# Windowed attention, mLSTM trunk: P^T V products in pairs, and K's low part on row halves in pairs

## The chip, the cores and the metric

One core of a Trainium2 chip runs the whole program. The metric is the device time of one execution in microseconds (us), the median of the runs; lower is better. The engines are named as in the profile: PE is TensorE's matmul, PEld its weight load, DVE is VectorE, ACT is ScalarE, POOL is GpSimd, SP issues DMAs.

## The reference, cut to what matters

Two sequences (2048 and 256 positions of 1024 values) go through an attention layer and an mLSTM layer, each with a residual, and a last RMS norm. The change lies in the attention layer alone:

```python
def window_attention_mixer(xn, w_in, sink, w_out):
    ...
    s = jnp.einsum('bnqgrd,bnkgd->bngrqk', qb, kb, preferred_element_type=jnp.float32)
    s = s * (ATTN_HEAD_DIM ** -0.5)
    ...
    m = jnp.maximum(jnp.max(s, axis=-1, keepdims=True), sk)
    p = jnp.exp(s - m)
    den = jnp.sum(p, axis=-1, keepdims=True) + jnp.exp(sk - m)
    p = (p / den).astype(vb.dtype)
    o = jnp.einsum('bngrqk,bnkgd->bnqgrd', p, vb).reshape(B, S, ATTN_WIDTH)
    return (o * jax.nn.silu(z)) @ w_out
```

There are 16 heads of 64 values in 4 groups; a group of 4 heads shares one K and one V. A block of 128 queries sees 3 blocks of keys (2 at the ends of a sequence).

## The kernel before, in words

The kernel works on 18 tiles of 128 positions (16 of the first sequence, 2 of the second), in stages: attention proper (`attn_core`), the gate and the output projection, and then the mLSTM layer. The change touches `attn_core` only.

In `attn_core` the projections (`project`, L376 to L378) multiply in three passes, since each operand is kept as a rounded high part and the rest as a low part: high by high, high by low, low by high. For a tile t there are four generators: `front(t + 2)` projects and rotates Q, K and V of a later tile; `scores` (letter s), `transposes` (p) and `values` (v) work on tile t. The string `AORDER` says in which order the program asks each for its next step. The tile framework then orders the instructions of each engine anew, with a model of their times, so that what stands next to what in an engine's queue is its choice; it may not break a dependence, and each buffer is one of a fixed number of copies.

`scores` (L489): for each of the 4 groups and each of its 4 heads, a PSUM tile S of 128 queries by up to 384 keys receives two passes, Q by KH (L500) and Q by KL (L501). Q holds 128 rows: for an even head rows 0 to 63 are the high part and rows 64 to 127 the low part, for an odd head the other way round (L454 to L457); KH and KL hold K's high and low part twice, in both row halves. So one pass of 128 rows gives the high and the low part of Q at once. There are two buffers "s", and in the last two tiles one more, "tq". VectorE adds the mask, takes the row's maximum and stores Sm (L503). After the fourth head it makes the group's nm (L508), ScalarE makes four exponentials in place (L514).

`transposes` (L522): for each group g and each key block j, four transposes (L528) fill one of two PSUM buffers "tr"; ScalarE (j = 0) or VectorE (else) copies it to PT (L531), one of NPT = 3 buffers. The order is all blocks of group 0, then all blocks of group 1, and so on.

`values` (L535): groups 2P and 2P + 1 share one PSUM tile o, one in partitions 0 to 63, the other in 64 to 127. For each block j and each of the two groups one product of V and PT (L541) is added; the operands are plain fp32, and each product stands as two passes in the trace. Then ScalarE copies o out (L544).

Of the kernel before, what the change touches and what calls it, by code (L numbers as in the profile page):

```python
# [11 lines left out]
F32 = mybir.dt.float32  # L12
# [31 lines left out]
NPT = 3  # L44
# [17 lines left out]
class Trunk:  # L62
# [330 lines left out]
    def attn_core(self):  # L393
        nc, tc, a = self.nc, self.tc, self.a
        with ExitStack() as st:
# [83 lines left out]
            def core(t):  # L479
# [9 lines left out]
                def scores():  # L489
                    for g in range(KVH):  # L490
                        mx = p.tile([128, 4], F32, tag="mx", name="mx", bufs=3)
                        Sg = []
                        for c in range(GRP):
                            h = g * GRP + c
                            Q = QS[t, h // 8]
                            q = Q[:, h % 2, (h % 8) // 2, :]
                            spare = NT - 2 <= t < SPT and c % 3 == 2
                            S = (pq if spare else ps).tile([128, 3, 128], F32, tag="tq" if spare else "s", name="s",
                                                           bufs=1 if spare else 2)
                            nc.tensor.matmul(S[:, :nk, :], q, KH[:, g, win, :], start=True, stop=False)  # L500
                            nc.tensor.matmul(S[:, :nk, :], q, KL[:, g, win, :], start=False, stop=True)  # L501
                            Sm = p.tile([128, 3, 128], F32, tag="Sm", name="Sm", bufs=NSM)
                            nc.vector.tensor_tensor_reduce(Sm[:, :nk], S[:, :nk], mask[:, t % 3, win, :], 1.0, MASKED,  # L503
                                                           ALU.add, ALU.max, mx[:, c:c + 1])
                            Sg.append(Sm)
# [16 lines left out]
                def transposes():  # L522
                    for g in range(KVH):
                        PTs[g] = []
                        for j in range(nk):
# [3 lines left out]
                            pt = p.tile([128, 512], F32, tag="PT", name="PT", bufs=NPT)  # L529
                            eng = nc.scalar.copy if j == 0 else nc.vector.tensor_copy  # L530
                            eng(pt[:], tp[:].rearrange("p c q -> p (c q)"))  # L531
                            PTs[g].append(pt)
                        yield

                def values():  # L535
                    for P in range(2):
                        o = ps.tile([128, 512], F32, tag="o", name="o", bufs=1)
                        for j in range(nk):
                            for gg in range(2):
                                g = 2 * P + gg  # L540
                                nc.tensor.matmul(o[gg * 64:(gg + 1) * 64, :], vof[sl[j]][:, g * HD:(g + 1) * HD],  # L541
                                                 PTs[g][j][:], start=j == 0, stop=j == nk - 1)
# [563 lines left out]
```

## Time and profile before

| | us |
|---|---|
| median of 3 runs | 2333.14 (2330.55 to 2336.04) |
| the profiled execution | 2326.69 |
| its span | 2324.8 |
| first and last product with V (L541) in it | 72.2 and 711.3 |
| mean granted clock of TensorE | 0.984 |

In the profile a row of a timeline holds start, duration, engine, line, operation, output and inputs, shape (rows by columns of the array, then the output) and count, and in brackets the engine's idle time before it with what ended it. TensorE overlaps its instructions: durations of matmuls are longer than the distance of their starts, and the distance is what a matmul costs. A window's row holds busy times of each engine, the granted clock, DMA share and GB/s.

### The profile page before, as it was taken

The page shows a single profiled execution, that of the slowest core. Times are in us where ns is not written, and L with a number is a line of the kernel's source. Part 1 is how long each engine was busy: PE and PEld are TensorE (multiplying, and loading weights), DVE is VectorE, ACT ScalarE, POOL GpSimd, SP SyncE. Part 2 cuts the span into 40 slices and gives each one's busy share as a digit, 9 for nine tenths or more (in the row PEclk, how much of TensorE's full clock was granted, in tenths as well). Part 3 has the DMA queues.
Part 4 walks back from the last instruction along what each step waited for, and adds up shares of the span by engine and source line. Part 5 has one row for each costly group of instructions (what it writes and reads, how often), then busy time and mean ns, then how long its engine had stood idle before and what let it go on. Part 6 is the DMA issues. An engine that isn't in the chain of part 4 may idle for free.

```text
span 2324.8 us, 32958 instructions
## 1 busy us (share of the span) xinstructions
PE 2239.7 (96%) x11102; PEld 1775.3 (76%) x11102; DVE 1564.6 (67%) x3403; ACT 1096.1 (47%) x2503; POOL 461.4 (20%) x392
## 2 busy tenths in 40 slices
PE   8999999999999998999899999999999996999998
PEld 7766666666666886888788899978877875888887
DVE  7575656565877779768655522397888786777784
ACT  6464545454765334445533411256454445554463
POOL 3212121212001221322000000012242234333320
PEclk9999999999999999999999999999999997999999
DMA  7111111111225447657533722354565457656642
GB/s 264 48 38 48 38 48 38 48 38 39 91 64 162 147 159 229 230 195 250 189 114 123 245 92 92 113 177 136 175 211 182 132 181 242 207 191 198 209 163 69
DMA packets 170281, 326.41 MB, mean 140 GB/s; under 512 B 18784, under 2 KB 21632, under 8 KB 170112
## 3 DMA queue, kind: packets, MB, share of 16 engines
q1 hardware_dynamic: 169968, 324.30, 42.0%
q8 instruction: 88, 1.44, 0.3%
q14 instruction: 81, 0.66, 0.1%
q10 hardware_dynamic: 144, 0.01, 0.0%
HBM read 235.34 MB, written 88.89 MB: 139 GB/s over the span
## 4 chain that ended last, share of the span: by engine, by line
PE 78%; DVE 8%; DMA 7%; issue 2%; ACT 2%; POOL 2%; SPq 0%; DVEq 0%; POOLq 0%; ACTq 0%
PE pj L378 9%; PE pj L376 9%; PE pj L377 9%; PE o L541 5%; PE pj L271 4%; PE pj L272 4%; PE pj L273 4%; PE ptp L528 4%; PE d L271 3%; PE d L272 3%; PE d L273 3%; PE c L272 3%; PE c L273 3%; PE c L271 3%; DMA qs<-rows 2%
## 5 line engine op out<-in xcount | busy, mean ns | idle before, releaser
L122 ACT CAST xhi<-rawx 128x512 fp32r<-128x512 f32 x372 | 228.6, 618 | 459.6 <-PE pj L377 109.0
L376 PE MATMUL pj<-whi,xhi 128*128 128x512 f32 (+2 forms) x1152 | 429.9, 374 | 8.5 <-ACT whi L167 6.9
L378 PE MATMUL pj<-whi,xlo 128*128 128x512 f32 (+2 forms) x1152 | 423.8, 373 | 5.8 <-DVE xlo L123 3.9
L377 PE MATMUL pj<-wlo,xhi 128*128 128x512 f32 (+2 forms) x1152 | 425.4, 369 | 0.0
L123 DVE TENSOR_TENSOR xlo<-rawx,xhi 128x512 fp32r<-128x512 f32 x338 | 247.6, 737 | 81.7 <-ACT xhi L122 73.9
L378 PEld LDWEIGHTS pj<-whi,xlo 128*128 128x128 f32 x1152 | 217.3, 189 | 56.1 <-issue 14.6
L376 PEld LDWEIGHTS pj<-whi,xhi 128*128 128x128 f32 x1152 | 217.4, 189 | 48.5 <-ACT whi L167 7.3
L377 PEld LDWEIGHTS pj<-wlo,xhi 128*128 128x128 f32 x1152 | 217.4, 189 | 37.4 <-issue 3.2
L271 PE MATMUL pj<-whi,xhi 128*128 128x512 f32 x480 | 194.3, 405 | 13.9 <-DVE x L612 8.9
L503 DVE CUSTOM_DVE_ANT_0 Sm<-s,mask 128x384 f32<-128x384 f32 (+1 forms) x272 | 137.7, 529 | 92.0 <-PE s L501 90.9
L514 ACT ACTIVATE Sm<-Sm,nm 128x384 f32<-128x384 f32 (+1 forms) x288 | 166.9, 581 | 68.2 <-DVE nm L508 67.0
L272 PE MATMUL pj<-wlo,xhi 128*128 128x512 f32 x480 | 192.7, 401 | 2.9 <-DVE wlo L190 2.9
L273 PE MATMUL pj<-whi,xlo 128*128 128x512 f32 x480 | 191.8, 400 | 0.0
L541 PE MATMUL o<-PT,V 128*64 128x512 f32 x400 | 148.0, 623 | 4.5 <-DVE PT L531 4.1
L528 PEld LDWEIGHTS ptp<-ident,Sm 128*128 128x128 f32 x800 | 94.3, 141 | 64.8 <-issue 31.2
L531 DVE COPY PT<-ptp 128x512 f32<-128x512 f32 x128 | 86.6, 686 | 71.8 <-PE ptp L528 37.7
L528 PE MATMUL ptp<-ident,Sm 128*128 128x128 f32 x800 | 127.9, 280 | 4.1 <-ACT Sm L514 1.7
L271 PE MATMUL d<-whi,xhi 128*128 128x512 f32 x320 | 128.1, 400 | 0.0
L272 PE MATMUL c<-wlo,xhi 128*128 128x512 f32 x320 | 127.2, 398 | 0.0
L273 PE MATMUL c<-whi,xlo 128*128 128x512 f32 x320 | 127.1, 397 | 0.0
L273 PE MATMUL d<-whi,xlo 128*128 128x512 f32 x320 | 127.0, 397 | 0.0
L271 PE MATMUL c<-whi,xhi 128*128 128x512 f32 x320 | 127.0, 397 | 0.0
(243 smaller groups left out, 4714.1 us busy)
## 6 DMA issues: line engine op xcount, KB each, us to landing
rawx<-xn2T SPq DMA_DIRECT2D x144, 256.0 KB, 3.1
x<-x SPq DMA_DIRECT2D x108, 256.0 KB, 3.8
rawx<-xT SPq DMA_DIRECT2D x72, 256.0 KB, 2.9
raww<-w_oz SPq DMA_DIRECT2D x64, 256.0 KB, 4.4
raww<-w_qkvg SPq DMA_DIRECT2D x40, 256.0 KB, 4.0
v<-v SPq DMA_DIRECT2D x18, 516.0 KB, 3.7
rawx<-v SPq DMA_DIRECT2D x36, 258.0 KB, 2.7
rawx<-x SPq DMA_DIRECT2D x36, 256.0 KB, 3.0
```

The costliest lines, as they stand in the source:

```text
L122: nc.scalar.copy(hi[:], src)
L123: (eng or nc.vector).tensor_sub(lo[:], src, hi[:].bitcast(F32))
L271: nc.tensor.matmul(o, xh, wh, start=i == 0 and not more, stop=False, skip_group_check=more)
L272: nc.tensor.matmul(o, xh, wl, start=False, stop=False, skip_group_check=more)
L273: nc.tensor.matmul(o, xl, wh, start=False, stop=i == 3, skip_group_check=more)
L376: nc.tensor.matmul(o[:, :n], xh, wh, start=kt == 0, stop=False)
L377: nc.tensor.matmul(o[:, :n], xh, wl, start=False, stop=False)
L378: nc.tensor.matmul(o[:, :n], xl, wh, start=False, stop=kt == KT - 1)
L503: nc.vector.tensor_tensor_reduce(Sm[:, :nk], S[:, :nk], mask[:, t % 3, win, :], 1.0, MASKED, ALU.add, ALU.max, mx[:, c:c + 1])
L514: nc.scalar.activation(Sg[c][:, :nk], Sg[c][:, :nk], AF.Exp, bias=nm[:, c:c + 1], scale=HD ** -0.5, accum_out=rs[:, c:c + 1])
L528: nc.tensor.transpose(tp[:, c, :], Ss[g][c][:, j, :], self.ident[:])
L541: nc.tensor.matmul(o[gg * 64:(gg + 1) * 64, :], vof[sl[j]][:, g * HD:(g + 1) * HD], PTs[g][j][:], start=j == 0, stop=j == nk - 1)
```

## The change

Three things change. In `scores`, two heads are taken together: the KL passes use only the 64 rows that hold Q's high part (rows 0 to 63 for the even head, 64 to 127 for the odd one), come first, and stand next to each other; the KH passes of both follow. The product of Q's low part with K's low part is left out by that. The two heads have a buffer each, s0 and s1. In `transposes`, the two groups of a pair P take turns, block by block, and NPT is 4. In `values`, the second group's product is issued first and the first group's is queued behind it (`tc.issue_after`: the instructions of its body are issued after the given one on that engine, without waiting for its end).

```diff
@@ -41,7 +41,7 @@
 WOPS = ("b11", "t2", "b21", "t3", "t1", "t4", "b22")
 PAIRS = [(t, t + 1) for t in range(0, NT, 2)]
 NSM = 11
-NPT = 3
+NPT = 4
 SPT = 18
 AORDER = "fffssssfsffffppsvppv"
 AORDER1 = "fffssssfsffffppsvppv"
@@ -489,20 +489,32 @@
                 def scores():
                     for g in range(KVH):
                         mx = p.tile([128, 4], F32, tag="mx", name="mx", bufs=3)
-                        Sg = []
+                        Sg, two = [], []
                         for c in range(GRP):
                             h = g * GRP + c
                             Q = QS[t, h // 8]
                             q = Q[:, h % 2, (h % 8) // 2, :]
                             spare = NT - 2 <= t < SPT and c % 3 == 2
-                            S = (pq if spare else ps).tile([128, 3, 128], F32, tag="tq" if spare else "s", name="s",
-                                                           bufs=1 if spare else 2)
-                            nc.tensor.matmul(S[:, :nk, :], q, KH[:, g, win, :], start=True, stop=False)
-                            nc.tensor.matmul(S[:, :nk, :], q, KL[:, g, win, :], start=False, stop=True)
-                            Sm = p.tile([128, 3, 128], F32, tag="Sm", name="Sm", bufs=NSM)
-                            nc.vector.tensor_tensor_reduce(Sm[:, :nk], S[:, :nk], mask[:, t % 3, win, :], 1.0, MASKED,
-                                                           ALU.add, ALU.max, mx[:, c:c + 1])
-                            Sg.append(Sm)
+                            S = (pq if spare else ps).tile([128, 3, 128], F32, tag="tq" if spare else f"s{c % 2}", name="s",
+                                                           bufs=1)
+                            two.append((S, q))
+                            if c % 2 == 0:
+                                continue
+
+                            def low(i):
+                                (S, q), rows = two[i], slice(i * 64, (i + 1) * 64)
+                                return nc.tensor.matmul(S[:, :nk, :], q[rows], KL[rows, g, win, :], start=True, stop=False)
+
+                            with tc.issue_after(low(1).ins):
+                                low(0)
+                                for S, q in two:
+                                    nc.tensor.matmul(S[:, :nk, :], q, KH[:, g, win, :], start=False, stop=True)
+                            for i, (S, _) in enumerate(two):
+                                Sm = p.tile([128, 3, 128], F32, tag="Sm", name="Sm", bufs=NSM)
+                                nc.vector.tensor_tensor_reduce(Sm[:, :nk], S[:, :nk], mask[:, t % 3, win, :], 1.0, MASKED,
+                                                               ALU.add, ALU.max, mx[:, c - 1 + i:c + i])
+                                Sg.append(Sm)
+                            two = []
                         hs = slice(g * GRP, (g + 1) * GRP)
                         nm = p.tile([128, 4], F32, tag="nm", name="nm", bufs=3)
                         nc.vector.scalar_tensor_tensor(nm[:], mx[:], -HD ** -0.5, nsink[:, hs], ALU.mult, ALU.min)
@@ -520,26 +532,29 @@
                         nc.vector.reciprocal(self.den[:, t, g // 2, :, g % 2], rs[:])
 
                 def transposes():
-                    for g in range(KVH):
-                        PTs[g] = []
-                        for j in range(nk):
+                    for P, j in product(range(2), range(nk)):
+                        for g in (2 * P, 2 * P + 1):
                             tp = ps.tile([128, 4, 128], F32, tag="tr", name="ptp", bufs=2)
                             for c in range(GRP):
                                 nc.tensor.transpose(tp[:, c, :], Ss[g][c][:, j, :], self.ident[:])
-                            pt = p.tile([128, 512], F32, tag="PT", name="PT", bufs=NPT)
+                            pt = PTs[g, j] = p.tile([128, 512], F32, tag="PT", name="PT", bufs=NPT)
                             eng = nc.scalar.copy if j == 0 else nc.vector.tensor_copy
                             eng(pt[:], tp[:].rearrange("p c q -> p (c q)"))
-                            PTs[g].append(pt)
-                        yield
+                        if j in (0, nk - 1):
+                            yield
 
                 def values():
                     for P in range(2):
                         o = ps.tile([128, 512], F32, tag="o", name="o", bufs=1)
+                        def half(j, gg):
+                            g = 2 * P + gg
+                            return nc.tensor.matmul(o[gg * 64:(gg + 1) * 64, :], vof[sl[j]][:, g * HD:(g + 1) * HD],
+                                                    PTs[g, j][:], start=j == 0, stop=j == nk - 1)
+
                         for j in range(nk):
-                            for gg in range(2):
-                                g = 2 * P + gg
-                                nc.tensor.matmul(o[gg * 64:(gg + 1) * 64, :], vof[sl[j]][:, g * HD:(g + 1) * HD],
-                                                 PTs[g][j][:], start=j == 0, stop=j == nk - 1)
+
+                            with tc.issue_after(half(j, 1).ins):
+                                half(j, 0)
                         ob = self.scr[:, P * 512:(P + 1) * 512]
                         nc.scalar.copy(ob, o[:])
                         nc.sync.dma_start(self.oT[t][:, P * 512:(P + 1) * 512], ob)
```

What this makes of TensorE's queue, at a place in the middle of the stage. The names are: ptp the transposes' PSUM tile, Sm the exponentials, s the scores, pqt the transposes of Q for a later tile, o the products with V. Before, at a group's first key block (ptp_2180) and what follows up to the next block of the same group:

```order
834 L528 MATMUL ptp_2180<-ident_60,Sm_1985 128x128
835 L528 MATMUL ptp_2180<-ident_60,Sm_1990 128x128
836 L528 MATMUL ptp_2180<-ident_60,Sm_1995 128x128
837 L528 MATMUL ptp_2180<-ident_60,Sm_2000 128x128
838 L541 MATMUL o_2201<-PT_2164,V_1254 64x512
839 L500 MATMUL s_2272<-KH_283,Q_1684 128x384
840 L501 MATMUL s_2272<-KL_284,Q_1684 128x384
841 L500 MATMUL s_2277<-KH_283,Q_1684 128x384
842 L501 MATMUL s_2277<-KL_284,Q_1684 128x384
843 L451 MATMUL pqt_2098<-ident_60,t1_2093 128x128 x4
844 L528 MATMUL ptp_2187<-ident_60,Sm_1985 128x128
845 L528 MATMUL ptp_2187<-ident_60,Sm_1990 128x128
```

The product with V at 838 stands alone, and a product, four score passes and four transposes lie between the group's first block and its second. After, TensorE at the same kind of place, where ptp_3303 is a second group's first block and ptp_3317 its second block:

```order
1333 L539 MATMUL ptp_3303<-ident_60,Sm_3135 128x128
1334 L506 MATMUL s_3410<-KL_284,Q_2821 128x384
1335 L506 MATMUL s_3409<-KL_284,Q_2821 128x384
1336 L511 MATMUL s_3409<-KH_283,Q_2821 128x384
1337 L511 MATMUL s_3410<-KH_283,Q_2821 128x384
1338 L539 MATMUL ptp_3303<-ident_60,Sm_3137 128x128
1339 L539 MATMUL ptp_3317<-ident_60,Sm_3125 128x128
1340 L539 MATMUL ptp_3317<-ident_60,Sm_3127 128x128
1341 L539 MATMUL ptp_3317<-ident_60,Sm_3135 128x128
1342 L539 MATMUL ptp_3317<-ident_60,Sm_3137 128x128
1343 L551 MATMUL o_3338<-PT_3308,V_2391 64x512
1344 L551 MATMUL o_3338<-PT_3301,V_2391 64x512
```

The KL passes and the products with V stand in pairs; nothing stands any more between the last transpose into ptp_3303 and the first into ptp_3317, which has the same PSUM buffer. ScalarE's queue at these two places (Q casts for a later tile, PT copies); before:

```order
194 L531 COPY PT_2164<-ptp_2159 128x512
195 L454 CAST Q_2063<-pqt_2058 64x512
196 L455 CAST Q_2063<-pqt_2058 64x512
197 L531 COPY PT_2185<-ptp_2180 128x512
198 L454 CAST Q_2103<-pqt_2098 64x512
```

And after:

```order
301 L523 ACTIVATE es_3141<-es_3141 128x4
302 L526 ACTIVATE Sm_3137,rs_3144<-Sm_3137,nm_3139 128x384
303 L454 CAST Q_3200<-pqt_3195 64x512
304 L455 CAST Q_3200<-pqt_3195 64x512
305 L542 COPY PT_3308<-ptp_3303 128x512
```

The copy stands behind two casts in both. Last, TensorE after the change at a place where a K pair follows a K pair:

```order
1366 L506 MATMUL s_3443<-KL_284,Q_2821 128x384
1367 L506 MATMUL s_3442<-KL_284,Q_2821 128x384
1368 L511 MATMUL s_3442<-KH_283,Q_2821 128x384
1369 L511 MATMUL s_3443<-KH_283,Q_2821 128x384
1370 L506 MATMUL s_3466<-KL_284,Q_2861 128x384
1371 L506 MATMUL s_3465<-KL_284,Q_2861 128x384
1372 L511 MATMUL s_3465<-KH_283,Q_2861 128x384
```

Before, two heads' passes there:

```order
854 L500 MATMUL s_2295<-KH_283,Q_1684 128x384
855 L501 MATMUL s_2295<-KL_284,Q_1684 128x384
856 L500 MATMUL s_2300<-KH_283,Q_1684 128x384
857 L501 MATMUL s_2300<-KL_284,Q_1684 128x384
858 L541 MATMUL o_2201<-PT_2192,V_1633 64x512
```

The second pair needs both buffers of the first, where each head needed one. From the output projection's stage on, the queues of all engines are the same in both kernels.

## Prediction

> **What bounds the kernel now.** I read first the busy table of the whole span, then the windows by stage, then TensorE's timeline inside the attention stage.
>
> ```profile
> span 2324.8 us, 32958 instructions
> ...
> PE 2239.7 (96%) x11102; PEld 1775.3 (76%) x11102; DVE 1564.6 (67%) x3403; ACT 1096.1 (47%) x2503; POOL 461.4 (20%) x392
> ```
>
> TensorE is the bound over the whole span. The change touches only the attention stage (first product with V at 72 us, last at 711 us); from the middle of the following stages on, the order of every engine is the same in both kernels. In the windows the columns are length, then busy time of PE, PEld, DVE, ACT and POOL, the granted clock, and DMA:
>
> ```profile
> 72.00:605.00 533.00, 529.64 (x2578) 365.45 (x2577) 327.31 (x966) 266.15 (x745) 93.01 (x80) 1.00 0.13 42
> 316.30:432.60 116.30, 115.63 (x566) 79.84 (x565) 70.91 (x211) 58.23 (x162) 20.82 (x18) 1.00 0.13 43
> 605.00:715.00 110.00, 100.89 (x468) 65.45 (x467) 85.68 (x263) 76.19 (x206) 6.19 (x4) 0.94 0.30 95
> ```
>
> The middle of the stage repeats every three tiles, in 116.3 us, of which TensorE idles 0.67 us (116.30 − 115.63). VectorE and ScalarE are busy 61% and 50%, so TensorE's issue times set the stage: what a group costs is read from start to start, not from the modelled durations. These are the rows for the products with V (L541; each product is two passes in the trace, so x2 is one product and x4 two):
>
> ```profile
> 302.22 1.08 PE L541 MATMUL o<-PT,V 128*64 128x512 f32 x4
> 303.23 0.50 PE L378 MATMUL pj<-whi,xlo 128*128 128x512 f32 x1
> 303.57 0.39 PE L376 MATMUL pj<-whi,xhi 128*128 128x512 f32 x1
> ...
> 307.05 0.40 PE L376 MATMUL pj<-whi,xhi 128*128 128x512 f32 x1
> 307.28 0.40 PE L377 MATMUL pj<-wlo,xhi 128*128 128x512 f32 x1
> 307.61 1.08 PE L541 MATMUL o<-PT,V 128*64 128x512 f32 x4
> ...
> 316.56 1.07 PE L541 MATMUL o<-PT,V 128*64 128x512 f32 x2
> 317.56 0.44 PE L500 MATMUL s<-KH,Q 128*128 128x384 f32 x1
> 317.84 0.33 PE L501 MATMUL s<-KL,Q 128*128 128x384 f32 x1
> 318.01 0.34 PE L500 MATMUL s<-KH,Q 128*128 128x384 f32 x1
> 318.19 0.34 PE L501 MATMUL s<-KL,Q 128*128 128x384 f32 x1
> 318.36 0.60 PE L451 MATMUL pqt<-ident,t 128*128 128x128 f32 x4
> 318.80 1.04 PE L528 MATMUL ptp<-ident,Sm 128*128 128x128 f32 x8
> ```
>
> Two neighbouring products take 1.01 us (302.22 to 303.23), one alone takes 1.00 us (316.56 to 317.56): the two halves of the array run at the same time, and a lone product wastes one half. Around each run of them something else is lost: the projection before takes 0.33 us instead of 0.23 (307.28 against 307.05), the one after 0.34 (303.23 to 303.57). A run therefore costs 1.00 + 0.10 + 0.11 = 1.21 us, single or paired. A score pass over 384 columns costs 0.175 us, four transposes 0.44 us (318.36 to 318.80).
>
> **Part 1, products with V in pairs.** TensorE's order holds 133 runs of V products before (70 of them a lone product) and 100 after (97 pairs). So 33 runs fall away: 33 × 1.21 = −40 us, and with the two runs of three −42 us. This saving is real only where TensorE is the bound and the pair finds both copies ready; the bound holds by the windows above, the copies are Part 3.
>
> **Part 2, K's low part on 64 rows.** 144 pairs of passes now run as two row halves side by side, between passes that use all 128 rows. Removed: one pass of each pair, 0.175 us for 112 pairs and 0.12 us for 32 pairs of 256 columns (645.53 to 645.65):
>
> ```profile
> 645.53 0.28 PE L500 MATMUL s<-KH,Q 128*128 128x256 f32 x1
> 645.65 0.28 PE L501 MATMUL s<-KL,Q 128*128 128x256 f32 x1
> ```
>
> That is 112 × 0.175 + 32 × 0.12 = −23 us, if switching were free. The only matmuls of the old trace on few rows surrounded by full ones are these of one row (L747):
>
> ```profile
> 1568.66 0.39 PE L273 MATMUL pj<-whi,xlo 128*128 128x512 f32 x1
> 1568.97 0.51 PE L747 MATMUL pl<-spr,ones 1*128 1x144 f32 x2
> 1569.41 0.50 PE L271 MATMUL pj<-whi,xhi 128*128 128x512 f32 x1
> 1569.75 0.40 PE L272 MATMUL pj<-wlo,xhi 128*128 128x512 f32 x1
> ```
>
> The pass before takes 0.31 us instead of 0.23 (+0.08; part of that may be its own wait), the pass after 0.34 (+0.11, 1569.41 to 1569.75), and the two small passes together 0.44. At V's pace (1.00 us for 2 × 512 columns at most) 2 × 144 columns need 0.24 to 0.28, so 0.16 to 0.20 more is lost inside. A visit to fewer rows costs about 0.08 + 0.18 + 0.11, say 0.39 us; from below it is bounded by zero (the free switch, a rival), from above by 0.39 plus a second weight load of 0.11. I take 0.39, because this row and the V rows agree on both edges although one cuts the array by rows and the other by columns. Then a pair costs 0.39 − 0.175 = +0.21 us (384) or +0.27 us (256): 112 × 0.21 + 32 × 0.27 = +32 us. In 24 places a V run and a K pair stand next to each other and share an edge (0.2 us): −5 us. Part 2 is +27 us.
>
> The Trainium skill speaks on both sides of this. "TensorEngine Tiling (Array Packing)", section Key Properties, says that changing the tiling mode drains the engine; the trace agrees by the two edges above. "TensorE: Matmul & The Clock Gate", Part 3, prices a packed group as one matmul plus about 4 ns for each further tile, with nothing for entering and leaving; by that rule alone Part 2 would be about −23 us instead of +27.
>
> Parts 1 and 2 together: −42 + 27 = −15 us, if TensorE never waited more than now.
>
> **Part 3, the waits that the new order brings.** NPT 4 costs nothing by itself (one more 128x512 buffer). The transposes now go through two heads' groups for one key block, then for the next, over the same two PSUM buffers ("tr"). So the transposes of the second group's second block reuse the buffer of its first block, which ScalarE has to copy out first. In the old order at least one other instruction stood between the two, usually five or more; in the new one they follow each other directly at 17 places (the front shows one). What TensorE waits there: at least the transpose's own latency and the copy, less the pace.
>
> ```profile
> 279.17 0.27 PE L528 MATMUL ptp<-ident,Sm 128*128 128x128 f32 x1
> ```
> ```profile
> 281.46 0.60 ACT L514 ACTIVATE Sm<-Sm,nm 128x384 f32<-128x384 f32 x1
> ...
> 283.26 0.19 ACT L511 ACTIVATE es<-es 128x4 f32<-128x4 f32 x1
> 283.36 0.56 ACT L454 CAST Q<-pqt 64x512 fp32r<-64x512 f32 x1
> 283.93 0.58 ACT L455 CAST Q<-pqt 64x512 fp32r<-64x512 f32 x1
> ...
> 285.73 0.58 ACT L531 COPY PT<-ptp 128x512 f32<-128x512 f32 x1
> ```
> ```profile
> 273.81 0.55 DVE L503 CUSTOM_DVE_ANT_0 Sm<-s,mask 128x384 f32<-128x384 f32 x1
> ...
> 274.29 0.69 DVE L436 TENSOR_TENSOR KL<-pk,KH 128x512 fp32r<-128x512 f32 x1
> 274.89 0.15 DVE L508 SCALAR_TENSOR_TENSOR nm<-mx,nsink 128x4 f32<-128x4 f32 x1
> ```
>
> Lower end: 0.27 + 0.58 − 0.11 = 0.74 us. Upper end, the whole chain, counted from the KH passes of the group's last pair: score ready 0.34; two reductions 2 × 0.48; KL 0.60 and nm 0.2 on VectorE; four exponentials 4 × 0.60 and es 0.1; two casts of Q, which stand ahead of the copy in ScalarE's order, 0.57 + 0.58; the copy 0.58: 6.3 us. TensorE meanwhile has 0.35 (KH) + 1.21 (V pair) + 0.44 (transposes of q) + 2 × 0.91 (K pairs with their KH: 0.39 + 0.175 + 0.35) + 8 × 0.11 = 4.7 us of work: wait 1.6 us. I take 1.3, nearer the chain, since the casts do stand ahead. Queued behind the waiting transposes are the V pair, the next K pair and at the end the projections; the reductions, and then the exponentials, wait for those. 17 × 1.3 = +22 us (13 to 27).
>
> Second wait: a K pair needs both score buffers, s0 and s1, and follows the pair before it directly in 5 places, with only four transposes between in 5. The release is quick, but the pair must be reduced whole:
>
> ```profile
> 125.13 0.45 PE L500 MATMUL s<-KH,Q 128*128 128x384 f32 x1 [0.31 <-DVE mx L503]
> ```
>
> From the first KH pass: 0.34 to the first score, 0.48 + 0.55 for two reductions and a release, about 1.4 us; TensorE's own 0.35 and the switch of 0.1 run meanwhile. 5 × 1.0 + 5 × 0.5 = +8 us (0 to 8; I take 7). Today's waits, 0.67 us in each of four three-tile periods, go into these: −3 us.
>
> Sum: −42 + 27 + 22 + 7 − 3 = **+11 us**. The profiled execution took 2326.69 us (span 2324.8 plus 1.9 around it), so 2337.7 us on its scale; the median shown is 2333.14, on which I forecast 2344 us. What lies behind the stage is late by the same amount, as TensorE is the bound there too.
>
> **The rivals.** (a) *The waits are covered: faster.* The mechanism is ScalarE arriving early at those 17 copies, with the Q casts done before the last transpose. For it: the old order had the casts ahead of the copy too and TensorE lost only 0.67 us in 116. Against: the old order had a V product, scores and transposes there as cover, the new has none, and even a free ScalarE needs 0.74 us. At 17 × 0.74 = 13 us and no second wait: −15 + 13 − 3 = −5; with the copies overlapping still more, −12: about 2324 for the middle. It decides at waits below 10 us in sum. (b) *Row halves switch free: faster.* Part 2 is then −23 instead of +27, and TensorE reaches the ScalarE chain earlier, which returns some 0.8 us at each of the 17 places (14 us): 11 − 50 + 14 = −25, 2308. Against it are the one-row rows. (c) *The change doesn't do what it says: the row halves run one after the other.* Weight load alone serial: 144 × 0.11 = 16 us; passes too: +23 us more. 2360 to 2383. For it: no row of the trace shows two row halves at once, only two column halves. (d) *Saving and waits cancel:* waits of about 15 us, 2333.
>
> **How the numbers follow.** Forecast 0.47, (a) 0.20, (b) 0.07, (c) 0.14, (d) 0.12. Slower is forecast and (c), 0.61; faster is (a) and (b), 0.27; same is (d), 0.12, where same is within 0.2%, 4.7 us, about what a measurement of this kernel can tell. The forecast's own ends are −15 + 13 + 0 − 3 = −5 and −15 + 27 + 8 = +20; the range goes down to 2318 to take in (a), and up to 2364 for the weight loads of (c); it leaves out (b) and the dearer half of (c).
>
> **What would show it.** In the new profile: V products in all but two cases as x4 with about 1.0 us; a K pair with its edges at about 0.56 us from start to start (right), near 0.2 (b), or 0.7 and more (c); idle before the ptp transposes put down to ScalarE's PT copy, 17 times about 1.3 us; idle before K pairs put down to the reductions; the period of three tiles near 119 us. A period under 115 us makes the forecast wrong, and the two idle groups say whether Part 3 or Part 2 failed.

## The result and the profile after

The changed kernel takes 2372.46 us (median of 4, 2364.23 to 2373.47) beside 2332.64 us for the kernel before in the same rounds (2330.55 to 2336.04): a ratio of 1.0162, with a 95% interval of 1.0136 to 1.0188. It is slower, as forecast, but by 40 us instead of 11, and 2372 lies above the range (2318 to 2364).

The page of the changed kernel shows TensorE as much the bound as before, with nearly the same busy time on every engine and a span that is longer:

```profile
span 2371.7 us, 32959 instructions
PE 2249.4 (95%) x11102; PEld 1754.4 (74%) x11102; DVE 1558.6 (66%) x3403; ACT 1098.3 (46%) x2503; POOL 464.2 (20%) x392
```

The windows of the changed kernel's attention stage (first product with V at 75.9 us, last at 750.8, against 72.2 and 711.3), and below them one period of three tiles. Columns as in the prediction:

```profile
72.00:640.00 568.00, 536.65 (x2600) 350.95 (x2599) 325.28 (x971) 270.19 (x744) 95.05 (x81) 0.98 0.12 40
640.00:760.00 120.00, 105.69 (x485) 65.06 (x484) 89.72 (x267) 79.94 (x216) 7.08 (x5) 0.90 0.30 96
```
```profile
302.24:424.95 122.71, 115.89 (x567) 75.93 (x565) 70.68 (x211) 58.65 (x163) 20.86 (x18) 0.99 0.13 41
```

Before, TensorE idled 12.5 us in the two windows of the stage (533.00 − 529.64 and 110.00 − 100.89); now 45.7 us (568.00 − 536.65 and 120.00 − 105.69). A period takes 122.7 us instead of 116.3, with 6.8 us idle instead of 0.7, while its busy time is the same (115.9 and 115.6). The last V product comes 39.5 us later than before (750.8 − 711.3), the first one 3.7 us, and the medians differ by 39.8. (The two spans differ by 46.9; the profiled execution of before was 6 us under its median.)

What TensorE waits for in the stage, by the view of waits. First the kernel before, then the changed one; the columns are microseconds in total, times, longest:

```profile
PE o L541 <- DVE PT L531: 4.1, 7, 1.3
PE s L500 <- DVE Q L457: 2.8, 1, 2.8
PE ptp L528 <- ACT Sm L514: 1.7, 2, 1.5
...
PE s L500 <- DVE mx L503: 0.8, 2, 0.5
PE ptp L528 <- ACT PT L531: 0.8, 1, 0.8
```
```profile
PE pqt L451 <- DVE nm L520: 14.9, 14, 1.7
PE s L506 <- DVE mx L514: 11.9, 23, 1.8
PE ptp L539 <- ACT PT L542: 10.3, 15, 0.7
PE ptp L539 <- ACT Sm L526: 1.9, 3, 1.5
```

Three groups of waits are new or many times longer: the transposes wait for ScalarE's copies (15 times, where the prediction listed 17 places), the K pairs for the reductions, and the transposes of Q (L451), which waited for nothing before, for VectorE.

The view of waits counts idle time from the modelled end of a matmul, so that a delay shorter than the overlap does not show. For a full account I summed, for each kernel, the distance from start to start that every matmul between the first and the last V product has when nothing is in its way, all from rows like those quoted: 0.454 ns a column for a rounded pass, 0.109 us a transpose, 0.854 us a V pair or lone product, with 0.15 us inside and 0.20 us on the neighbours for each run of them; for a K pair its columns once and 0.195 us, and 0.20 us on the neighbours. What the stage takes beyond this sum is called waits from here on:

| kernel | stage, us | sum without waits | waits |
|---|---|---|---|
| before | 639.9 | 615.3 | 24.6 |
| after | 675.9 | 600.0 | 75.9 |

So the prices fell by 15.3 us (forecast 15), and the waits rose by 51 us (forecast 26).

Not all of these 51 us are waiting. The sum takes the prices at full clock, and TensorE did not always have it: the granted clock of the windows above is 1.00 and 0.94 before, 0.98 and 0.90 after. In the trace it falls to 0.5 for some us at a time, for 13.7 us of the stage before and for 43.9 us after. There a projection takes 0.43 us from start to start, and 0.23 when the clock is back (a window of 3 us in such a stretch, and TensorE's timeline around it):

```profile
223.30:226.30 3.00, 3.00 (x8) 2.36 (x8) 2.97 (x9) 2.53 (x9) 1.28 (x2) 0.50 0.00 0
```
```profile
222.46 0.45 PE L506 MATMUL s<-KL,Q 64*128 64x384 f32 x2 [0.96 <-DVE mx L514]
...
224.20 0.63 PE L378 MATMUL pj<-whi,xlo 128*128 128x512 f32 x1
224.62 0.63 PE L376 MATMUL pj<-whi,xhi 128*128 128x512 f32 x1
225.05 0.63 PE L377 MATMUL pj<-wlo,xhi 128*128 128x512 f32 x1
...
227.17 0.39 PE L377 MATMUL pj<-wlo,xhi 128*128 128x512 f32 x1
227.40 0.39 PE L378 MATMUL pj<-whi,xlo 128*128 128x512 f32 x1
```

At most half of that time is lost by the clock, 7 us before and 22 us after (an estimate; TensorE also idled in some of it). So up to 15 of the 51 us are slower matmuls, and 36 us or more are waits proper. The mean clock of the four executions of the changed kernel agrees, 0.975 to 0.977 beside 0.984 of the profiled one before. No run changed the clock alone, so what lowers it stays open.

By the instruction that waits, the waits of after, with the clock's part in them, are 26.4 us at the transposes of the scores (8.8 before), 23.4 at K pairs and the KH passes behind them (9.6 at the passes of the scores before), 17.3 at L451 (none before).

One burst of the changed kernel shows how these hang together. Its timeline, with TensorE, VectorE and ScalarE:

```profile
328.82 0.40 PE L377 MATMUL pj<-wlo,xhi 128*128 128x512 f32 x1
329.06 0.39 PE L378 MATMUL pj<-whi,xlo 128*128 128x512 f32 x1
...
329.38 0.45 PE L506 MATMUL s<-KL,Q 64*128 64x384 f32 x2
...
329.76 0.62 PE L511 MATMUL s<-KH,Q 128*128 128x384 f32 x2
...
330.24 0.56 DVE L514 CUSTOM_DVE_ANT_0 Sm<-s,mask 128x384 f32<-128x384 f32 x1 [4.23 <-PE s L511]
...
330.31 1.08 PE L551 MATMUL o<-PT,V 128*64 128x512 f32 x4
...
330.72 0.56 DVE L514 CUSTOM_DVE_ANT_0 Sm<-s,mask 128x384 f32<-128x384 f32 x1
...
331.20 0.69 DVE L436 TENSOR_TENSOR KL<-pk,KH 128x512 fp32r<-128x512 f32 x1
...
331.80 0.15 DVE L520 SCALAR_TENSOR_TENSOR nm<-mx,nsink 128x4 f32<-128x4 f32 x1
...
331.99 0.61 ACT L526 ACTIVATE Sm<-Sm,nm 128x384 f32<-128x384 f32 x1
...
332.03 0.63 PE L451 MATMUL pqt<-ident,t 128*128 128x128 f32 x4 [0.64 <-DVE nm L520]
...
333.90 0.60 ACT L526 ACTIVATE Sm<-Sm,nm 128x384 f32<-128x384 f32 x1
...
334.50 0.56 ACT L454 CAST Q<-pqt 64x512 fp32r<-64x512 f32 x1
334.54 0.19 PEld L506 LDWEIGHTS s<-KL,Q 64*128 64x128 f32 x2 [0.43 <-DVE mx L514]
334.54 0.44 PE L506 MATMUL s<-KL,Q 64*128 64x384 f32 x2 [0.20 <-DVE mx L514]
...
335.67 0.59 ACT L542 COPY PT<-ptp 128x512 f32<-128x512 f32 x1
...
336.31 0.66 PE L539 MATMUL ptp<-ident,Sm 128*128 128x128 f32 x4 [0.68 <-ACT PT L542]
```

The K pair costs what was forecast: 0.32 us from the projection before it (0.23 undisturbed), 0.38 to the KH passes. The chain of the prediction is there too, from the KH passes at 329.76 over the reductions, KL, nm, the exponentials, the casts of Q and the copy to the transposes at 336.31: 6.5 us, where 6.3 were forecast. But TensorE pays in three places, 0.64 + 0.20 + 0.68 = 1.5 us, and only the last stood in my list.

### The profile page after: what moved, and what is told of

It is laid out like the page before. It is cut to its first block, busy times and chain, and to the rows that moved or that the text cites. A ratio compares the mean times of both kernels' runs of the same rounds, so it can differ in the third digit from the quotient of the medians.

```text
span 2371.7 us, 32959 instructions
## 1 busy us (share of the span) xinstructions
PE 2249.4 (95%) x11102; PEld 1754.4 (74%) x11102; DVE 1558.6 (66%) x3403; ACT 1098.3 (46%) x2503; POOL 464.2 (20%) x392
## 4 chain that ended last, share of the span: by engine, by line
PE 78%; DVE 9%; DMA 5%; ACT 4%; issue 2%; POOL 2%; SPq 0%; DVEq 0%; POOLq 0%; ACTq 0%
PE pj L376 9%; PE pj L378 9%; PE pj L377 9%; PE pj L271 4%; PE pj L272 4%; PE pj L273 4%; PE o L551 4%; PE ptp L539 3%; PE c L271 3%; PE c L272 3%; PE c L273 3%; PE d L271 3%; PE d L272 3%; PE d L273 3%; PE s L511 2%
## 5 line engine op out<-in xcount | busy, mean ns | idle before, releaser
L376 PEld LDWEIGHTS pj<-whi,xhi 128*128 128x128 f32 x1152 | 218.6, 190 | 53.5 <-issue 8.1
L539 PE MATMUL ptp<-ident,Sm 128*128 128x128 f32 x800 | 135.0, 288 | 13.4 <-ACT PT L542 10.3
L272 PE MATMUL d<-wlo,xhi 128*128 128x512 f32 x320 | 127.3, 398 | 0.0
L271 PEld LDWEIGHTS pj<-whi,xhi 128*128 128x128 f32 x480 | 92.1, 192 | 38.8 <-ACT whi L189 13.4
```

The lines of the kernel that those rows point to most:

```text
L271: nc.tensor.matmul(o, xh, wh, start=i == 0 and not more, stop=False, skip_group_check=more)
L272: nc.tensor.matmul(o, xh, wl, start=False, stop=False, skip_group_check=more)
L376: nc.tensor.matmul(o[:, :n], xh, wh, start=kt == 0, stop=False)
L539: nc.tensor.transpose(tp[:, c, :], Ss[g][c][:, j, :], self.ident[:])
```

## The experiments

Twelve kernels were run. Each ratio, with its interval, is against the kernel before on the same chip; two kernels are compared by their ratios, times 2332 us, since the runs of before shift by some us from one set to the next. At the end of the section one table has the account of all of them. Where an expectation speaks of waits, it means what lies beyond the prices, the clock's part included.

**v_alone**: only the products with V in pairs, with the new order of the transposes and NPT 4.

```diff
-NPT = 3
+NPT = 4
...
-                    for g in range(KVH):
...
-                        for j in range(nk):
+                    for P, j in product(range(2), range(nk)):
+                        for g in (2 * P, 2 * P + 1):
...
+                            with tc.issue_after(half(j, 1).ins):
+                                half(j, 0)
```

> The pairs of products with V alone: transposes block by block, NPT 4 and issue_after in values as in the changed kernel, scores as in the kernel before. Theory (saving and cost as priced: V runs save about 42 us without waits, the loss comes with the K pairs and their waits): 99 runs of V instead of 133, 9 places where the second block's transposes directly follow the first's (0.7 us each): 2297 to 2312 us, about 2304. Rival 1 (the waits come with the pairing of V and the new order of the transposes): no gain, 2325 to 2345. Rival 2 (V runs save only their lone halves hidden elsewhere): within 5 us of 2333.

Measured: 2318.79 us, ratio 0.9946 (0.9928 to 0.9964), between the theory and rival 1. Faster, but by 13 us where the prices fall by 44: 35 us of them came back as waits, more than expected, although the scores are untouched. The clock has no part in that: it is at 0.5 for 13.7 us of the stage, as before.

**k_alone**: only the scores by two heads with K's low part on row halves (the change's `scores`, the rest as before).

> The score pairs with K's low part on 64 rows alone; transposes, values and NPT 3 as before. Theory: switching the rows +32 us without waits, less 2 us for 10 runs of V fewer, and waits of K pairs for their two buffers and of the transposes of Q: +15 to +30; 2377 to 2392 us. Rival 1 (most waits come with the transposes' order): +30 and few waits, 2355 to 2367. Rival 3 (row switching costs little, waits only): 2340 to 2355.

Measured: 2370.02 us, ratio 1.0172 (1.0153 to 1.0191), between the theory and rival 1. The sum without waits is 25.8 us above that of before (Part 2 of the prediction said +27), and the waits rise by 10 us.

**full_rows**: the changed kernel with K's low part again on all 128 rows, everything else kept (two heads together, pairs, order).

```diff
-                                (S, q), rows = two[i], slice(i * 64, (i + 1) * 64)
+                                (S, q), rows = two[i], slice(0, 128)
```

> The changed kernel, with both KL passes over all 128 rows again: pairs, order, two buffers s0 and s1, V pairs all as changed, but no switch to row halves. It adds Q's low part times K's low part as the kernel before does. Theory: the switch's +27 us goes, waits stay or grow a little since TensorE arrives earlier: 2342 to 2352 us. Rival 2 (the switch carries all of the loss): 2300 to 2325, as good as V alone. Rival 3 (the lockstep of two score buffers carries it): 2360 or more.

Measured: 2342.71 us, ratio 1.0051 (1.0035 to 1.0068), as expected. The row halves alone cost the changed kernel 26 us by the ratios (30 by the medians, 26.9 in the stage). The waits seem to stay (77.5 us here, 75.9 in the changed kernel), but the clock is at 0.5 for 15.1 us of the stage here and for 43.9 us there. Without the clock's part, up to 14 us more there, the waits proper are up to 16 us shorter with the row halves than without. By this estimate part of their price did hide in the waits, and the lower clock took about as much back. So taking two heads' scores together, without any switch, already costs 24 us against v_alone (2342.7 and 2318.8), 18 of them in waits.

**no_pk**: the changed kernel, but VectorE no longer reads the PSUM buffer that the transposes of K and those of Q share. KL becomes KH − KH, that is, K's low part is left out of the result.

```diff
-                nc.vector.tensor_sub(KL[:, :, s, :], pk[:], KH[:, :, s, :].bitcast(F32))
+                nc.vector.tensor_sub(KL[:, :, s, :], KH[:, :, s, :].bitcast(F32), KH[:, :, s, :].bitcast(F32))
```

> The changed kernel, with KL computed as KH minus KH instead of pk minus KH, so that VectorE no longer reads the transposes of K in PSUM; K's low part is zero by that and left out of the scores. The 14 waits of Q's transposes (L451, 1.06 us each) are put down to VectorE's nm. Theory: they wait for the PSUM buffer that the KL subtraction, just ahead of nm on VectorE, still reads; without that read they go and the time falls by 8 to 15 us, 2357 to 2364. Rival: they wait for nm itself, or for GpSimd's sum of the rotated Q: unchanged waits, 2368 to 2375.

Measured: 2380.75 us, ratio 1.0216 (1.0198 to 1.0235): slower, above both the theory and the rival. Its waits:

```profile
PE ptp L539 <- ACT Sm L526: 16.4, 21, 1.5
PE s L506 <- DVE mx L514: 12.7, 15, 1.2
...
PE pqt L451 <- ACT KH L435: 4.5, 6, 0.8
```

The 14.9 us of L451 against nm are gone, and the exponentials' 1.9 us have become 16.4. In sum the waits are 78.1 us instead of 75.9. The framework ordered this kernel's instructions anew, so the two are not the same program but for one wait. The run speaks against VectorE's read of this one buffer as the place where the time is lost; alone it does not settle it.

**copy_split**: the changed kernel with another engine for the copies. Of the second group of each pair VectorE copies the first block, ScalarE the second.

```diff
-                            eng = nc.scalar.copy if j == 0 else nc.vector.tensor_copy
+                            eng = nc.scalar.copy if j == g % 2 else nc.vector.tensor_copy
```

> The changed kernel, but of each pair of head groups the second has its first block's PT copied by VectorE and its second block's by ScalarE; the transposes that follow directly (17 places) then wait for VectorE instead of ScalarE. Theory A (one buffer, kept by a ScalarE that is late by its casts of Q): the 10.3 us that stand against ScalarE's PT copy go and little comes in their place, 2360 to 2366. Theory B: they move to VectorE's PT copy and to the reductions behind it, 2368 to 2378.

Measured: 2371.58 us, ratio 1.0178 (1.0161 to 1.0196), the time of the changed kernel, as theory B has it. Its waits:

```profile
PE ptp L539 <- DVE PT L542: 15.8, 17, 1.0
PE pqt L451 <- DVE nm L520: 14.9, 14, 1.7
PE s L506 <- DVE mx L514: 11.6, 27, 1.0
PE ptp L539 <- ACT Sm L526: 7.8, 9, 1.4
```

The 17 direct successions now wait for VectorE, and longer. Theory A in the form in which it was put, a ScalarE that is late with one buffer, falls here: it is not that engine's copy. (This kernel, too, was ordered anew.)

**v_oldorder**: V in pairs, but the transposes in their old order (all key blocks of a group, then the next group) and NPT 6; scores as before.

```diff
-NPT = 3
+NPT = 6
...
-                            for gg in range(2):
-                                g = 2 * P + gg
-                                nc.tensor.matmul(o[gg * 64:(gg + 1) * 64, :], vof[sl[j]][:, g * HD:(g + 1) * HD],
-                                                 PTs[g][j][:], start=j == 0, stop=j == nk - 1)
+                            with tc.issue_after(half(j, 1).ins):
+                                half(j, 0)
```

> Products with V in pairs, but the transposes in the old order (a head group's three key blocks one after the other) and six PT buffers; scores as before. TensorE's order then holds 101 turns of V products in 83 runs, against 136 in 133 before: 35 x 1.00 + 50 x 0.21 = -46 us without waits. Theory A (the waits of the changed kernel come from the new order of the transposes, a group's second block directly behind its first over the same two buffers): there is no such place here, the waits in the attention stage stay near the 25 us of before, 2333 - 46 = 2287, with up to 10 us more waits 2287 to 2297. Theory B (the waits are what the chain reduction, exponential, transpose, copy on VectorE and ScalarE is longer than TensorE's work in a burst, whatever the order): less work on TensorE lengthens them as it did with V pairs alone (44 us saved, 35 waited again), so 2310 to 2325.

Measured: 2285.27 us, ratio 0.9803 (0.9786 to 0.9820), just below theory A's numbers. A period of three tiles of this kernel:

```profile
309.64:417.83 108.19, 108.10 (x566) 78.68 (x565) 67.51 (x211) 58.30 (x162) 20.82 (x18) 1.00 0.15 46
```

TensorE idles 0.09 us in 108. Theory B, that less work on TensorE only lengthens its waits, falls here: 52 us of prices are gone and the waits are 27.0 us, against 24.6 before. It is the fastest of the twelve.

**after_oldorder**: the changed kernel with the old order of the transposes and NPT 6.

> The changed kernel with the transposes in the old order and six PT buffers: 104 turns of V in 79 runs (32 x 1.00 + 54 x 0.21 = -43 us against before), K's low part on row halves as changed (+26 us): -17 us without waits. Theory A: the transposes' waits fall back from 26 to about 9 us and the others stay, so the waits are 45 to 60 instead of 76, and the time 2333 - 17 + 20 to 35 = 2336 to 2351. Theory B: the waits stay at 70 to 80 us and only change their names, 2333 - 17 + 45 to 55 = 2361 to 2371.

Measured: 2343.92 us, ratio 1.0061 (1.0044 to 1.0077): theory A's numbers again, 24 us less than the changed kernel (29 in the stage). The waits are 51.1 us. They were expected to fall at the transposes; they fell most at L451 (from 17.3 to 6.9), and only from 26.4 to 22.3 at the transposes.

**t_order**: the new order of the transposes and NPT 4 alone; V products not tied together, scores as before.

> Only the new order of the transposes and four PT buffers; products with V not tied together, scores as before. TensorE's order then holds 172 turns of V products in 171 runs, 143 of them lone: 36 x 1.00 + 38 x 0.21 = +44 us without waits, 2377. Both theories: the price of a run is tested, 1.21 us for a lone product as for a pair. Theory A adds no waits (one direct place): 2372 to 2382. Theory B: the added work on TensorE covers waits, 10 to 20 of the 25 us of before, so 2357 to 2367.

Measured: 2380.22 us, ratio 1.0218 (1.0202 to 1.0233). The framework then lays 143 of 171 runs as lone products, and the stage's prices rise by 44.8 us, as the 1.21 us of a run said (+44). Waits rise by 7 us only, although the order of the transposes is the new one. That a lone product can be issued as soon as its own copy is there, and fills what a pair has to wait for, is my reading; no run shows it by itself.

**v_old4 and v_alone6** separate the order from the number of buffers: v_oldorder with NPT 4, and v_alone with NPT 6.

> V in pairs and the old order of the transposes as in v_oldorder, with four PT buffers instead of six: 101 turns of V in 87 runs (35 x 1.00 + 46 x 0.21 = -45 us without waits against before). It has the same buffers as v_alone, so that only the order of the transposes differs. Theory A (the order makes the waits): waits 25 to 35 us, 2285 to 2298. Rival (six buffers made v_oldorder fast, not the order): waits near the 59 us of v_alone, 2312 to 2325.

> V in pairs and the new order of the transposes as in v_alone, with six PT buffers instead of four: 100 turns in 99 runs, the same as v_alone. Theory A (the order makes the waits): within 4 us of v_alone, 2314 to 2322. Rival (the number of buffers): waits fall to 25 to 35 us, 2284 to 2297.

Measured: 2295.34 us for v_old4, ratio 0.9841 (0.9826 to 0.9855), and 2315.66 us for v_alone6, ratio 0.9927 (0.9911 to 0.9944). With four buffers the order is worth 24 us (0.9946 − 0.9841), with six 29 (0.9927 − 0.9803). Two more buffers are worth 9 us in the old order and 4 in the new, the latter within the intervals. Theory A holds by the times (the waits of v_old4, 38.7 us, are a little above its 25 to 35); the buffers are a smaller, second term.

**full_rows_old**: after_oldorder with K's low part on all 128 rows. (The remark on the output in what was expected is mistaken: the other 64 rows hold Q's low part, and the pass is that of the kernel before.)

> after_oldorder with K's low passes on all 128 rows again (the upper 64 rows only repeat what the lower have, so the output differs in size): scores still in lockstep by two heads, V in pairs, old order of the transposes, six PT buffers. Theory C (visiting row halves costs 144 x 0.2 us on TensorE, not covered by waits): the time falls by 26 to 32 us from after_oldorder, 2312 to 2318. Rival (part of the visit's cost hides in the waits of the lockstep, which grow when TensorE has less to do): 2322 to 2334. What then remains above v_oldorder's 2285 is the price of the lockstep.

Measured: 2318.29 us, ratio 0.9944 (0.9929 to 0.9959), between the two expectations. The row halves cost 27 us here by the ratios (24.9 in the stage), of 32 that the prices say; the waits are 7 us less with them, although the clock is at 0.5 for 33.0 us of the stage with them and for 22.9 us without. And it is 33 us above v_oldorder, with the same sum without waits (563.7 and 563.3): taking the scores of two heads together costs 31 us of waits, up to 6 of them by the clock (10.2 us at 0.5 in v_oldorder). The waits of full_rows_old:

```profile
PE s L506 <- DVE mx L514: 10.3, 18, 0.9
PE pqt L451 <- DVE nm L520: 8.7, 5, 1.8
PE ptp L540 <- ACT Sm L526: 5.9, 5, 2.5
```

**v_noexp**: v_alone, with the exponentials written to a buffer of their own and the transposes reading the masked scores, so that they no longer wait for the exponentials. The result is not attention.

```diff
-                            nc.scalar.activation(Sg[c][:, :nk], Sg[c][:, :nk], AF.Exp, bias=nm[:, c:c + 1],
+                            E = p.tile([128, 3, 128], F32, tag="E", name="E", bufs=2)
+                            nc.scalar.activation(E[:, :nk], Sg[c][:, :nk], AF.Exp, bias=nm[:, c:c + 1],
...
-MASKED = -1e30
+MASKED = -1.0
```

> v_alone (V in pairs, new order of the transposes, four PT buffers), but the exponentials write to a buffer of their own and the transposes take the masked scores as they are, so that they wait for the reductions and not for ScalarE's exponentials; ScalarE does the same work as before. The output is not attention: products of V are made with scores that were not exponentiated, and the masked value is -1. Theory A (the new order asks for both groups' exponentials before the first pair of V, and TensorE waits for them and for the copies that stand behind them on ScalarE): the waits of 59 us fall to 25 to 40, 2284 to 2300. Rival (the waits come from the reductions, the copies and the buffers alone): 45 to 60 us remain, 2305 to 2320.

Measured: 2289.30 us, ratio 0.9811 (0.9790 to 0.9832), theory A's numbers. TensorE's work is the same (570.9 and 571.8 us without waits), ScalarE does the same exponentials, and the waits fall from 59.5 to 26.3 us. Only the dependence of the transposes on the exponentials is gone, and with it the whole loss of v_alone. Part of that may come through the framework, which ordered this kernel anew too (the nine direct successions of v_alone are gone).

The account of the attention stage, worked out for each as above. The last but one column is the time for which the profiled execution had the granted clock at 0.5 in the stage; up to half of it is part of the waits:

| kernel | scores | transposes, PT buffers | sum without waits | waits | clock at 0.5, us | ratio to before |
|---|---|---|---|---|---|---|
| before | single | old, 3 | 615.3 | 24.6 | 13.7 | 1 |
| v_oldorder | single | old, 6 | 563.3 | 27.0 | 10.2 | 0.9803 |
| v_noexp | single | new, 4 | 571.8 | 26.3 | 10.2 | 0.9811 |
| v_old4 | single | old, 4 | 564.4 | 38.7 | 19.6 | 0.9841 |
| v_alone6 | single | new, 6 | 570.9 | 56.7 | 10.2 | 0.9927 |
| full_rows_old | two heads | old, 6 | 563.7 | 58.3 | 22.9 | 0.9944 |
| v_alone | single | new, 4 | 570.9 | 59.5 | 13.7 | 0.9946 |
| full_rows | two heads | new, 4 | 571.5 | 77.5 | 15.1 | 1.0051 |
| after_oldorder | row halves | old, 6 | 595.8 | 51.1 | 33.0 | 1.0061 |
| after | row halves | new, 4 | 600.0 | 75.9 | 43.9 | 1.0162 |
| k_alone | row halves | old, 3 | 641.1 | 34.8 | 20.5 | 1.0172 |
| copy_split | row halves | new, 4 | 598.8 | 82.4 | 47.0 | 1.0178 |
| no_pk | row halves | new, 4 | 602.9 | 78.1 | 27.3 | 1.0216 |
| t_order | single | new, 4 | 660.1 | 31.6 | 3.4 | 1.0218 |

By the four that lie on one path from before to after: pairs of V in the old order with four buffers −37 us (v_old4), the new order of the transposes +24 (v_alone), two heads' scores together +24 (full_rows), row halves +26 (after). That is +37, and the ratio of after says +38; each step is known to some 5 us.

## Why the prediction was right in sign and wrong in size

*What bounds the kernel* held: every kernel's time follows TensorE's prices, its waits and its clock in the stage.

*Part 1* held. 100 runs at 1.21 us; the price is shown a second time by t_order, where 38 more runs cost what they should. What I did not see is that the same pairs were to be had in the old order, at 52 us instead of 44.

*Part 2* held as a price: 0.37 us for the visit, of which 0.175 are its columns, and about 0.20 us on its two neighbours, so 0.39 us lost a visit, as forecast; in sum +26 us by k_alone and +28.5 by after against full_rows (600.0 − 571.5), where +27 was forecast. That the time also moves by 26 us from full_rows to after is in part luck: the waits proper got up to 16 us shorter and the clock cost up to 14 us more, and neither was in the forecast. The nearest rows that I had, a visit to a single row and V's visits to half the columns, priced a visit to half the rows rightly. The Trainium skill prices a packed group as one matmul and some nanoseconds for each further tile ("TensorE: Matmul & The Clock Gate", Part 3). The trace agrees that the two matmuls run at once, their starts 3 to 4 ns apart; as the price of the whole visit, with nothing for entering and leaving, it does not hold here, where 0.39 us a visit are lost. What the Trainium skill says of a change of the tiling mode, that it drains TensorE ("TensorEngine Tiling (Array Packing)", Key Properties), agrees with the losses on both edges.

*Part 3* failed, most of all in its second wait, "a K pair needs both score buffers" (+7, at most 8): taking two heads together costs 24 us in the new order and 33 in the old. Beside the path above, the terms of the forecast are −42 for the pairs of V (measured −37), +27 for the row halves (+26), +22 for the new order (+24), and +7 − 3 for the score buffers less today's waits (+24). Of the 26 us between the two sums, 20 lie in the last term. In the account of the stage, the waits of Part 3 were +26 and the runs have +51, of which up to 15 are the granted clock, a term that the prediction put at nothing. Three things were wrong with the waits.

First, I listed places instead of following the chain. I looked for where the order put a waiting instruction straight behind what it waits for, found the 17 transposes, priced the chain from the scores to the copy rightly (6.5 us measured, 6.3 forecast), and put the whole lateness there. In the burst above TensorE loses the 1.5 us in three places, and the first of them, the transposes of Q at L451, was not in my list at all: 17.3 us in the stage, none before. In the burst VectorE reads the PSUM buffer that they take (L436, at 331.20) only behind two reductions that start on one pair.

Second, the cause that I gave for the +22, a buffer that ScalarE frees late, is not the cause, and that the size came out near the 24 us of the order is luck. With the copy on VectorE the time stays (copy_split), and with another wait removed the sum stays (no_pk). With the old order (v_old4 against v_alone) or without the wait for the exponentials (v_noexp) the loss goes. The new order needs the exponentials of two groups before the first pair of V. By the trace the transposes then run close behind them: of the 72 head groups' first transposes, those that start less than 0.25 us after the group's last exponential ended are 14 before, 17 in v_old4 and 42 in v_alone. The fourth group of a tile does so in 17 of 18 tiles in v_alone and in 5 in v_old4, which is what the order explains: four transposes stand between it and the third group's start instead of twelve. That the first group does it too (16 of 18, against 10) is not explained by it, and I have no run on it. Nor is the order enough by itself: in t_order, with lone products and 89 us more of prices than v_alone, 30 first transposes stand as close, 13 of them of fourth groups, and the waits are 31.6 us. Together with pairs of V the order costs 24 us; with lone products the waits rose by 7.

Third, the second wait (+7) was priced by the 10 places where a K pair stands close behind another. Taking two heads together costs 18 us of waits in the new order and 31 in the old, without any row half. The view of waits puts it on the reductions, L451 and the exponentials. That two reductions start together, later than the first of them did, is my reading of it; no run changed that alone, so it stays argued.

Of the rivals, (c) had 2360 to 2383 and so the time, with a wrong mechanism: the two row halves of a pair start 3 to 4 ns apart and run at once. (b) and (d) are refuted by k_alone and by the waits. (a) is what a different edit gives: with the old order the waits stay near those of before (27.0 and 24.6 us), and the pairs of V make the kernel 2% faster.

## What to carry to other kernels

Price a new order by what it has to have ready first, not by the buffers that it takes: a step that joins two groups makes the later group's whole chain a condition for the first of it, and the lateness then shows up at whatever instruction happens to stand there. A wait that moves to another name when its engine or buffer is changed points to a chain behind it, and not to that engine or buffer. And before what lies beyond the prices is called a wait, look at the granted clock: here it was up to 15 us of 51. When one edit brings a gain and carries a reordering with it, try the gain without the reordering: here the pairs in the old order gave 1.6% with four PT buffers and 2% with six.

## What the runs showed of the hardware

Two matmuls on the two row halves start 3 to 4 ns apart and take the columns' time once. The price is in the switch: 0.10 us on the pass before, some 0.20 us in the visit beyond its 0.175 us of columns, 0.10 us on the pass after. The edges are the same for V's cut by columns, where some 0.15 us are lost inside. A visit pays here only if it saves more than 0.4 us; one pass of 384 columns is 0.175 us.

TensorE's granted clock falls to 0.5 for stretches of 3.4 to 13.7 us within the stage, and a projection of 512 columns then takes 0.43 us instead of 0.23. In both pairs of kernels whose programs differ by the row halves alone, these stretches are longer with them: 43.9 us against 15.1 (after and full_rows) and 33.0 against 22.9 (after_oldorder and full_rows_old). The length of the waits does not set it: full_rows and v_alone, with waits of 77.5 and 59.5 us, have 15.1 and 13.7 us of it, and the kernel before, with 24.6, has 13.7. One execution of each was profiled, and the cause is not shown.

By the same estimate as above the waits cover part of the row halves' price. In the stage 28.5 us of prices came with up to 16 us less of waits proper and up to 14 us more of clock, and the stage grew by 26.9; in the old order 32.1 us came with up to 12 us less and 5 more, and it grew by 24.9.
